# Two more stores whose last two heads go to the first four DMA engines, with the next store held until the other heads have landed

## The chip, the cores and the metric

One core of one Trainium2 chip. The metric is the device time of one execution in microseconds (us). All executions quoted are of the fast state. A ratio is the mean time of one kernel's fast runs over the mean of the other's fast runs of the same rounds on the same chip, so it is not quite the ratio of the medians quoted beside it; intervals are 95%.

## The reference, cut to what matters

```python
# q, k: (16, 512, 16, 64) float32 = batch, sequence, heads, dim; cos, sin: (512, 32)
q_rot = concat([q1*cos - q2*sin, q1*sin + q2*cos])      # the same for k
scores = np.einsum('bshd,bthd->bsht', q_rot, k_rot)     # (16, 512, 16, 512) float32
```

The output is 268 MB and the inputs are 67 MB. The kernel is a long stream of stores with some loads between them.

## The kernel before

The work is cut into 64 steps, four per batch. A step rotates queries and keys (VectorE), transposes them and forms the scores of 128 sequence rows for 16 heads (TensorE), copies them from PSUM into one of three staging buffers of 4 MB (ScalarE), and stores that buffer. SyncE issues all of these transfers. The third and the fourth step of each batch are followed by a load of 2 MB of queries and of keys.

```python
stage_pool = ctx.enter_context(tc.tile_pool(name="stage", bufs=3))
...
    def store(i, st):
        o = o_v[i // C, i % C]
        if i not in (NST - 8, NST - 1):          # NST = 64: steps 56 and 63
            nc.sync.dma_start(o, st)
            return

        h = H - 2
        nc.sync.dma_start(o[:, :h], st[:, :h])
        nc.sync.dma_start(o[:116, h:], st[:116, h:])
        nc.sync.dma_start(o[116:, h:], st[116:, h:])
...
        for i in range(C, NST):
            ...
            st = stage_pool.tile([P, H, S], fp32, tag="stage", name="st")
            for p in range(HP):
                scores(i, p, st)                  # the last of them calls store(i, st)
                ...
            run(dve)
            if i % C == C - 2:
                load("q", i // C + 2)
            elif i % C == C - 1:
                load("k", i // C + 3)
```

A whole store gives each of the 16 DMA engines eight row packets of 32 KB. An **uneven** store gives each engine eight packets of 28 KB (14 heads), then 29 packets of 4 KB to each of the first four engines (116 rows of two heads), then one 4 KB packet to each of the first twelve. I call the 29 packets the four engines' **rest**. It is meant to take load off the slower engines among the other twelve.

Of the kernel before, what the change touches and what calls it, by code (L numbers as in the profile page):

```python
# [10 lines left out]
def kernel(  # L11
# [8 lines left out]
    nc = tc.nc  # L20
# [4 lines left out]
    B, S, H, D = q.shape  # L25
    HD = D // 2
    P = 128
    C = S // P
    HP = H // 2
    NST = B * C  # L30
    G = H // C

    const_pool = ctx.enter_context(tc.tile_pool(name="const", bufs=1))
# [13 lines left out]
    o_v = out.rearrange("b (p c) h t -> b c p h t", c=C)  # L47
# [14 lines left out]
    def load_units(which, head, heads):  # L62
        n = C * heads * D
        t = early[:, used[0] : used[0] + n].rearrange("p (c e) -> p c e", c=C)
        used[0] += n
        src = dram[which][0, :, :, head : head + heads, :]
        nc.sync.dma_start(t.rearrange("p c (h d) -> p c h d", d=D), src)
        for h in range(0, heads, G):
            units[which, (head + h) // G] = t[:, :, D * h : D * (h + G)]

    batches = {}

    def load(which, b):

        if b >= B:
            return
        t = in_pool.tile([P, C, H * D], fp32, tag=which + "_in", name=which + "_sb")
        batches[which, b] = t
        nc.sync.dma_start(t.rearrange("p c (h d) -> p c h d", h=H), dram[which][b])

    def rope(which, n):


        part = part_pool.tile([P, H * D], fp32, tag="part", name="part")
        if n < C:
            x = units[which, n]
            sv, k1, k2 = "p c (g j) -> p c g j", {"j": HD}, {"j": D}
            cs = cos_t.unsqueeze(2).to_broadcast((P, C, 2 * G, HD))
            ss = ss_v.unsqueeze(2).to_broadcast((P, C, G, D))
            pv = part.rearrange("p (c g j) -> p c g j", c=C, j=D)  # L90
            x5 = x.rearrange("p c (h x j) -> p c h x j", x=2, j=HD)
            p5 = part.rearrange("p (c h x j) -> p c h x j", c=C, x=2, j=HD)
            adds = [(x5[:, :, :, y], p5[:, :, :, 1 - y]) for y in range(2)]
        else:
            x = batches[which, n // C][:, n % C]
            sv, k1, k2 = "p (g j) -> p g j", {"j": HD}, {"j": D}
            cs = cos_t[:, n % C].unsqueeze(1).to_broadcast((P, 2 * H, HD))
            ss = ss_v[:, n % C].unsqueeze(1).to_broadcast((P, H, D))
            pv = part.rearrange(sv, **k2)
            x4 = x.rearrange("p (h x j) -> p h x j", x=2, j=HD)  # L100
            swapped = bass.AP(part.tensor, part.offset + HD, [part.ap[0], (D, H), (-HD, 2), (1, HD)])
            adds = [(x4, swapped)]
        xs, xc = x.rearrange(sv, **k2), x.rearrange(sv, **k1)

        def products():
            nc.vector.tensor_tensor(pv, xs, ss, op=mult)  # L106
            nc.vector.tensor_tensor(xc, xc, cs, op=mult)  # L107

        def sums():
            for y, z in adds:  # L110
                nc.vector.tensor_tensor(y, y, z, op=add)  # L111

        return [products, sums]
# [4 lines left out]
    def transposed(which, n, g, copy):  # L118
# [22 lines left out]
                dst = kT[b][:, 4 * g : 4 * g + 4, P * (n % C) : P * (n % C + 1)]  # L141
        copy(out=dst, in_=src)  # L142

    def store(i, st):
        o = o_v[i // C, i % C]
        if i not in (NST - 8, NST - 1):
            nc.sync.dma_start(o, st)
            return

        h = H - 2  # L150
        nc.sync.dma_start(o[:, :h], st[:, :h])
        nc.sync.dma_start(o[:116, h:], st[:116, h:])
        nc.sync.dma_start(o[116:, h:], st[116:, h:])

    def scores(i, p, st):

        ps = ps_s_pool.tile([P, 2, S], fp32, tag="ps_s", name="ps")
        b = i // C
        if b == 0:
            c, hp = divmod(p, 2)  # L160
            lhs, rhs = qT[i][:, C * hp + c], kT[0][:, 2 * i + hp]
        else:
            lhs, rhs = qT[i][:, p], kT[b][:, p]
        for r in range(2):
            po, rh = ps[:, r, :], rhs[64 * r : 64 * r + 64, :]
            nc.tensor.matmul(  # L166
                out=po, lhsT=lhs[64 * r : 64 * r + 64, :], rhs=rh, start=True, stop=True
            )
        so, si = st[:, 2 * p : 2 * p + 2, :], ps
        if b > 0:  # L170
            so = so.rearrange("s r (t c) -> s r t c", c=C)
            si = si.rearrange("s r (c t) -> s r t c", c=C)
        nc.scalar.copy(out=so, in_=si)  # L173
        if b == 0 and p % 2 == 1:
            c = p // 2
            nc.sync.dma_start(o_v[0, c, :, G * i : G * (i + 1)], st[:, G * c : G * (c + 1)])
        elif b > 0 and p == HP - 1:
            store(i, st)

    def tr_act(which, n):  # L180
        for g in range(2):
            transposed(which, n, g, nc.scalar.copy)

    def run(ops):
        for op in ops:
            op()

    with tc.manual_schedule():
        for t, src in ((cos_t, cos), (sin_t, sin)):
            nc.scalar.dma_start(t, src.rearrange("(p c) j -> p c j", c=C))  # L190
        for head, heads in ((0, G), (G, H - G)):
            load_units("k", head, heads)
            load_units("q", head, heads)
        load("k", 1)
        load("q", 1)
        make_identity(nc, ident)
        nc.scalar.copy(out=ss_t[:, :, 0, :], in_=sin_t)
        nc.scalar.mul(ss_t[:, :, 1, :], sin_t, -1.0)
        for which in ("k", "q"):
            run(rope(which, 0))  # L200
            tr_act(which, 0)


        for i in range(C):
            st = st_first[i] if i < 2 else stage_pool.tile([P, H, S], fp32, tag="stage", name="st")
            if i < C - 1:
                dve = rope("k", i + 1) + rope("q", i + 1) + rope("k", C + i)
                nxt = [("k", i + 1), ("q", i + 1)]
            else:
                dve = rope("q", C) + rope("k", C + i) + rope("q", C + 1) + rope("k", 2 * C)  # L210
                nxt = [("q", C), ("k", C + i)]
            for p in range(HP):
                scores(i, p, st)
                if p in (0, 1) and i > 0:
                    run(dve[:1])
                    dve = dve[1:]
                    transposed("k", C + i - 1, p, nc.vector.tensor_copy)
                if p == 3 and i < 2:
                    load("kq"[i], 2)
                if p in (2, 6):  # L220
                    m = len(dve) - (4 if p == 2 else 2) - (2 if i == C - 1 else 0)
                    run(dve[:m])
                    dve = dve[m:]
                    tr_act(*nxt.pop(0))
            run(dve)
        load("k", 3)


        for i in range(C, NST):
            tr = {}  # L230
            if i + 1 < NST:
                tr[1], tr[3] = ("q", i + 1, 0), ("q", i + 1, 1)
            if i + C < NST:
                tr[5], tr[6] = ("k", i + C, 0), ("k", i + C, 1)
            dve = []
            if i + 2 < NST:
                dve += rope("q", i + 2)
            if i + 1 + C < NST:
                dve += rope("k", i + 1 + C)
            st = stage_pool.tile([P, H, S], fp32, tag="stage", name="st")  # L240
            for p in range(HP):
                scores(i, p, st)
                if p not in tr:
                    continue
                if tr[p][0] == "q":
                    run(dve[:1])
                    dve = dve[1:]
                    transposed(*tr[p], nc.vector.tensor_copy)
                else:
                    transposed(*tr[p], nc.scalar.copy)  # L250
            run(dve)
            if i % C == C - 2:
                load("q", i // C + 2)
            elif i % C == C - 1:
                load("k", i // C + 3)


# [28 lines left out]
```

## Time and profile before

| | before |
|---|---|
| time, median of 5 runs beside the changed kernel | 799.13 us (798.6 to 799.73) |
| span of the profiled execution | 799.5 us |
| last landing of step 63's 14 heads, one engine alone | 798.27 us |
| last landing of step 63's rest, four engines | 796.32 us |

The lines of the profile on which the argument rests are shown in the prediction. The last two rows come from the trace's completion records: each engine's share of a transfer has a time of its own, so one can see which share landed first and which last. The profiled execution of the kernel before took 801.33 us in all, 2.2 us above its median. I call the engine that lands last the laggard, and the bunch that lands first the quick engines.

### The profile page before, as it was taken

The page shows a single profiled execution, that of the slowest core. Times are in us where ns is not written, and L with a number is a line of the kernel's source. Part 1 is how long each engine was busy: PE and PEld are TensorE (multiplying, and loading weights), DVE is VectorE, ACT ScalarE, POOL GpSimd, SP SyncE. Part 2 cuts the span into 40 slices and gives each one's busy share as a digit, 9 for nine tenths or more (in the row PEclk, how much of TensorE's full clock was granted, in tenths as well). Part 3 has the DMA queues.
Part 4 walks back from the last instruction along what each step waited for, and adds up shares of the span by engine and source line. Part 5 has one row for each costly group of instructions (what it writes and reads, how often), then busy time and mean ns, then how long its engine had stood idle before and what let it go on. Part 6 is the DMA issues. An engine that isn't in the chain of part 4 may idle for free.

```text
span 799.5 us, 7719 instructions
## 1 busy us (share of the span) xinstructions
PE 688.9 (86%) x3072; PEld 299.3 (37%) x3072; DVE 544.5 (68%) x516; ACT 561.4 (70%) x647; POOL 0.7 (0%) x6
## 2 busy tenths in 40 slices
PE   4989998988979889698897989979979799798970
PEld 2444443433424334243343433424434244343420
DVE  6999987667857667576685766857758577586300
ACT  3888886867848668586685867857757577577870
POOL 0000000000000000000000000000000000000000
PEclk9999999999989989999898989988989889899995
DMA  9999999999999999999999999999999999999996
GB/s 350 423 425 423 434 425 433 424 434 433 420 441 421 439 425 427 436 427 432 428 429 430 434 420 430 425 434 428 403 430 434 436 410 416 430 425 381 422 439 261
DMA packets 17988, 336.17 MB, mean 420 GB/s; under 512 B 1824, under 2 KB 3104, under 8 KB 4384
## 3 DMA queue, kind: packets, MB, share of 16 engines
q1 hardware_dynamic: 17664, 335.55, 98.7%
q8 instruction: 24, 0.39, 0.2%
q10 hardware_dynamic: 288, 0.13, 0.1%
q14 instruction: 12, 0.10, 0.0%
HBM read 67.24 MB, written 268.44 MB: 420 GB/s over the span
## 4 chain that ended last, share of the span: by engine, by line
DMA 48%; PE 38%; DVE 5%; ACT 5%; issue 1%; ACTq 0%; DVEq 0%
DMA out_dram<-st 48%; PE ps L166 28%; PE bank L127 9%; ACT st L173 5%; DVE part L106 2%; DVE early L111 1%; DVE k_sb L111 1%; DVE k_sb L107 1%; DVE early L107 1%; DMA early<-in_k_dram 1%; DVE kT_t L142 0%; DVE q_sb L107 0%; DVE q_sb L111 0%; ACTq L281 0%; DVE qT_t L142 0%
## 5 line engine op out<-in xcount | busy, mean ns | idle before, releaser
L173 ACT COPY st<-ps 128x1024 f32<-128x1024 f32 x512 | 494.8, 1019 | 203.2 <-DMA out_dram<-st 108.6
L166 PE MATMUL ps<-kT_t,qT_t 64*128 64x512 f32 x2048 | 545.8, 650 | 72.5 <-ACT st L173 72.5
L166 PEld LDWEIGHTS ps<-kT_t,qT_t 64*128 64x128 f32 x2048 | 184.5, 197 | 261.3 <-issue 140.3
L142 DVE COPY qT_t<-bank 128x512 f32<-128x512 f32 x118 | 81.5, 691 | 203.9 <-PE bank L127 203.9
L127 PEld LDWEIGHTS bank<-ident,q_sb 128*128 128x128 f32 x480 | 56.0, 153 | 103.1 <-issue 100.5
L127 PE MATMUL bank<-ident,q_sb 128*128 128x128 f32 x480 | 87.6, 310 | 0.9 <-PE ps L166 0.9
L127 PEld LDWEIGHTS bank<-ident,k_sb 128*128 128x128 f32 x480 | 50.5, 141 | 94.3 <-DVE k_sb L107 35.4
L127 PE MATMUL bank<-ident,k_sb 128*128 128x128 f32 x480 | 78.7, 287 | 1.6 <-DVE qT_t L142 1.2
L142 ACT COPY kT_t<-bank 128x512 f32<-128x512 f32 x122 | 72.5, 598 | 6.4 <-PE bank L127 6.4
L107 DVE TENSOR_TENSOR q_sb<-q_sb,cos_t 128x1024 f32<-128x1024 f32 x60 | 73.5, 1225 | 2.1
L107 DVE TENSOR_TENSOR k_sb<-k_sb,cos_t 128x1024 f32<-128x1024 f32 x60 | 73.5, 1225 | 2.0
L111 DVE TENSOR_TENSOR k_sb<-k_sb,part 128x1024 f32<-128x1024 f32 x60 | 73.5, 1225 | 2.1
L106 DVE TENSOR_TENSOR part<-q_sb,ss_t 128x1024 f32<-128x1024 f32 x60 | 73.5, 1225 | 2.0
L106 DVE TENSOR_TENSOR part<-k_sb,ss_t 128x1024 f32<-128x1024 f32 x60 | 72.9, 1215 | 0.1
L111 DVE TENSOR_TENSOR q_sb<-q_sb,part 128x1024 f32<-128x1024 f32 x60 | 72.9, 1215 | 0.0
L127 PE MATMUL bank<-ident,early 128*128 128x128 f32 x64 | 10.5, 316 | 12.3 <-DVE early L111 10.4
L127 PEld LDWEIGHTS bank<-ident,early 128*128 128x128 f32 x64 | 8.3, 161 | 17.4 <-issue 14.8
L106 DVE TENSOR_TENSOR part<-early,ss_t 128x1024 f32<-128x1024 f32 x8 | 9.8, 1222 | 5.8 <-DMA early<-in_k_dram 5.6
L111 DVE TENSOR_TENSOR early<-early,part 128x512 f32<-128x512 f32 x16 | 10.3, 687 | 0.2
L107 DVE TENSOR_TENSOR early<-early,cos_t 128x1024 f32<-128x1024 f32 x8 | 9.8, 1226 | 0.3
L142 ACT COPY qT_t<-bank 128x512 f32<-128x512 f32 x10 | 5.7, 617 | 3.2 <-PE bank L127 3.2
L142 DVE COPY kT_t<-bank 128x512 f32<-128x512 f32 x6 | 4.1, 684 | 0.9 <-PE bank L127 0.9
(9 smaller groups left out, 2.8 us busy)
## 6 DMA issues: line engine op xcount, KB each, us to landing
out_dram<-st SPq DMA_DIRECT2D x58, 4096.0 KB, 24.0
k_sb<-in_k_dram SPq DMA_DIRECT2D x15, 2048.0 KB, 27.9
q_sb<-in_q_dram SPq DMA_DIRECT2D x15, 2048.0 KB, 28.3
out_dram<-st SPq DMA_DIRECT2D x16, 1024.0 KB, 13.5
out_dram<-st SPq DMA_DIRECT2D x2, 3584.0 KB, 23.9
early<-in_k_dram SPq DMA_DIRECT2D x1, 1536.0 KB, 8.7
early<-in_q_dram SPq DMA_DIRECT2D x1, 1536.0 KB, 12.0
out_dram<-st SPq DMA_DIRECT2D x2, 464.0 KB
```

The lines of the kernel that those rows point to most:

```text
L106: nc.vector.tensor_tensor(pv, xs, ss, op=mult)
L107: nc.vector.tensor_tensor(xc, xc, cs, op=mult)
L111: nc.vector.tensor_tensor(y, y, z, op=add)
L127: nc.tensor.transpose(bank[:, x, :], src, ident)
L142: copy(out=dst, in_=src)
L166: nc.tensor.matmul(out=po, lhsT=lhs[64 * r : 64 * r + 64, :], rhs=rh, start=True, stop=True)
L173: nc.scalar.copy(out=so, in_=si)
```

## The change

The intent: relieve the laggard at two more steps, and let the four engines do their rest while the others would wait. Steps 31 and 43 become uneven as well. Their rest is now issued after the load of that step, and the next store (32, 44) is held on SyncE until all shares of the 14-head store have landed. Only SyncE's order of instructions differs.

```diff
+    UNEVEN = (31, 43, 56, NST - 1)
...
+    stores = {}
+    held = mybir.DependencyInfo(mybir.DependencyClass.Sync, mybir.DependencyReason.ANTI)
     def store(i, st):
         o = o_v[i // C, i % C]
-        if i not in (NST - 8, NST - 1):
-            nc.sync.dma_start(o, st)
-            return
-        h = H - 2
-        nc.sync.dma_start(o[:, :h], st[:, :h])
-        nc.sync.dma_start(o[:116, h:], st[:116, h:])
-        nc.sync.dma_start(o[116:, h:], st[116:, h:])
+        h = H - 2 if i in UNEVEN else H
+        stores[i] = nc.sync.dma_start(o[:, :h], st[:, :h])
+        if i - 1 in UNEVEN and i % C == 0 and i < NST - C:
+            tc.add_manual_dep(stores[i].ins, stores[i - 1].ins.name, held, reason="lead")
+    def rest_of_store(i, st):
+        if i in UNEVEN:
+            for rows in (slice(0, 116), slice(116, P)):
+                nc.sync.dma_start(o_v[i // C, i % C, rows, H - 2 :], st[rows, H - 2 :])
...
             elif i % C == C - 1:
                 load("k", i // C + 3)
+            rest_of_store(i, st)
```

## The prediction

> **What bounds the kernel now.** I read the page first (busy shares, slices, DMA queues), then the chain of waits, then windows, then the trace's completion records. The page:
>
> ```profile
> PE 688.9 (86%) x3072; PEld 299.3 (37%) x3072; DVE 544.5 (68%) x516; ACT 561.4 (70%) x647; POOL 0.7 (0%) x6
> DMA  9999999999999999999999999999999999999996
> q1 hardware_dynamic: 17664, 335.55, 98.7%
> q8 instruction: 24, 0.39, 0.2%
> out_dram<-st SPq DMA_DIRECT2D x58, 4096.0 KB, 24.0
> ```
>
> See here: the transfers of queue q1 take 98.7% of the span on the mean of 16 engines, so no compute engine is the bound; only the last slice falls, to six tenths. A mean cannot say which of the 16 ends last. The windows say a little about that (columns: window, length, busy time of PE, PEld, DVE, ACT and POOL, granted clock, DMA share, GB/s):
>
> ```profile
> 500.00:600.00 100.00, 88.42 (x388) 37.78 (x386) 68.78 (x66) 70.14 (x81) 0.00 (x0) 0.91 1.00 424
> 728.00:730.00 2.00, 2.00 (x11) 0.96 (x12) 1.93 (x3) 1.91 (x3) 0.00 (x0) 1.00 0.69 295
> 730.00:732.00 2.00, 2.00 (x12) 0.78 (x8) 1.97 (x2) 1.85 (x4) 0.00 (x0) 1.00 0.42 180
> 732.00:734.00 2.00, 2.00 (x14) 1.00 (x12) 1.17 (x3) 1.61 (x2) 0.00 (x0) 1.00 1.12 475
> ...
> 792.00:794.00 2.00, 0.00 (x0) 0.00 (x0) 0.00 (x0) 0.00 (x0) 0.00 (x0) 0.50 0.40 150
> 794.00:796.00 2.00, 0.00 (x0) 0.00 (x0) 0.00 (x0) 0.00 (x0) 0.00 (x0) 0.50 0.33 119
> 796.00:798.00 2.00, 0.00 (x0) 0.00 (x0) 0.00 (x0) 0.00 (x0) 0.00 (x0) 0.50 0.04 18
> ```
>
> See the one large hole, at 728 to 732 us, and the tail: at 792 to 794 us 0.40 of 16, some six engines, still move data; at 796 to 798 us 0.04, one engine. So the time is set by the **slowest single engine**, not by the mean. The chain of waits shows how the program follows it:
>
> ```profile
> 399.67 0.33 SPq L147 DMA_DIRECT2D out_dram<-st  x1
> 400.11 0.98 SPq L79 DMA_DIRECT2D k_sb<-in_k_dram  x1
> 409.69 24.49 SPq L147 DMA_DIRECT2D out_dram<-st  x3
> ...
> 409.69 28.29 DMA out_dram<-st
> 437.98 0.02 issue
> 438.00 0.04 ACTq L173
> ```
>
> The first three lines are SyncE's timeline (store of step 31, load of keys, store of step 32 and two more), the rest the chain: a store is issued at 409.69, its last share lands at 437.98, and only then does ScalarE get that staging buffer back.
>
> The completion records hold a time for each engine's share of a transfer. For the store of step 31: first share at 413.86 us, last at 423.05; in order, 0.0 0.0 0.0 0.0 0.1 0.5 0.6 0.7 0.9 1.2 2.2 4.4 5.3 5.7 7.8 9.2 us after the first. Eleven engines run nearly together and five lag, the last by 9.2 us. This spread was 0.7 us at the early loads, 4.4 at step 4, 11.5 at step 42, and 11.8 at step 56. The laggard is never without work; the eleven begin to be: their landings against an unbroken sum of packets slip by 0.4 us near 516, 1.7 near 561, 2.1 near 660, and over 4 us at the hole of 728 to 732, where they wait for the store of step 58.
>
> **What the Trainium skill says.** "DMA: Bandwidth & Descriptors", section "Why a DMA increments its semaphore by 16 and not by 1": a transfer is spread over the largest k up to 16 that divides its slowest dimension, and from SyncE these are the lowest-numbered k. 116 rows give k = 4 (29 rows each), 12 rows give k = 12. The trace agrees: 4 and 12 completions. Same page, "Anatomy of one DMA": waits are made by the issuing sequencer, the engines just consume their queues; so the new hold blocks SyncE only, and queued transfers go on. The trace agrees: after a dry spell, the store issued at 731.80 lands first at 742.75, which is eight packets of 1.21 us and 1.25 us to start and report. "Runtime: NRT & Kernel Launch", "Instruction fetch mechanics": instructions come in 16 KiB blocks over a DMA queue of their own. The trace agrees: q8 moves 24 such blocks, some 0.94 us each, on whichever engines; part of why engines are unequal.
>
> **The change, part by part.** Nothing moves on PE, VectorE or ScalarE; the order of instructions differs on SyncE alone, by four more issues (116 and 12 rows, twice, behind the load of that step) and a wait before the stores of steps 32 and 44. Steps 56 and 63 were uneven already.
>
> *For the twelve others, the laggard among them.* A row packet of 32 KB takes 1.213 us, one of 28 KB 1.062, one of 4 KB 0.159. One uneven store: 8 x 0.151 = 1.21 us less, for the laggard one 4 KB packet more, so -1.04. (Of the twelve completions for 12 rows at step 56, the last came at 729.9, behind its other shares, so the laggard is among engines 4 to 11.) Twice: **-2.1 us on the laggard**, whose last landing moves from 798.46 to 796.4.
>
> *For the first four.* 29 x 0.159 = 4.61, plus 0.17 for the twelfth rows and semaphores, less 1.21: +3.6 us, twice **+7.2 us**. At step 56 their four landings came 4.66, 4.8, 5.2 and 6.0 us after the first main landing: they are among the quick eleven, but one is 1.3 us behind. Now they finish at 796.65. Their slack is what they idle: 0.4 + 1.7 + 2.1 = 4.2 us, and at most 0.6 us at 728 to 732 (there they still had step 56's rest to do, ending store 57 at 732.4 to 733.8 against data at 733.05). 796.65 + 7.2 - 4.2 = **799.6 us**, 1.2 us after the present end of 798.46.
>
> *The hold.* The slow share of store 31 now lands at 423.05 - 1.2 = 421.9; store 32 is then issued and its data flows at about 423.1. The laggard still has 4.85 us of keys until 426.9: no hole for it, with 3.8 us to spare. The quick ones without rest are done at 418.7 - 1.2 = 417.5 and idle 5.6 us, which costs nothing as they are ahead by more. The four run their rest from 417.5 to 422.4 (the hindmost to 423.6) and idle 0.7 us at most. At step 43 the lead is smaller, the four run past the release and idle nothing. The 12-row packet behind the keys gives buffer 31 back at 427.0 instead of 423.05, so step 34's store goes from 433.9 to about 437.9; two stores, some 19 us, are queued then, so this is hidden.
>
> Sum: the end is the later of laggard (796.4) and the four (799.6), against 798.46: +1.2 us, and 799.13 + 1.2 = 800.3 us.
>
> **Rivals.** (1) *The laggard stays the bound*: the four keep up because they idle more before than I count. Then the whole -2.1 us comes through: 797.0 us. For it: the end of the run before is a lone engine from 796.7 on, and the change is visibly meant for this. Against: the four need 7.2 us and I find under 5. (2) *The four become the bound*, my sum: 800.3, up to 802 if the hindmost of them, which idled less, decides, or if the laggard is less slow in unprofiled executions (the profiled one took 801.33 us against 799.13), so that there is less to win. (3) *The hold opens a hole on all 16*: for it, the late buffer 31 and a store issued 12 us later; against, the 3.8 us to spare and 19 us in queue. If a hole opens it is some 2 to 4 us each time: 803 to 807. (4) All cancels, since the two ends differ by a few us and laggards wander: 799.
>
> **Range and chances.** I give (1) 0.35, (2) 0.4, (4) 0.2, (3) 0.05. 0.35 x 797.0 + 0.4 x 800.6 + 0.2 x 799.1 + 0.05 x 805 = 799.2; I take 799.4. Eight in ten: 796.9 to 801.6. Two per cent are 16 us; every term here is under 8 us, so faster 0.005, same 0.985, slower 0.01.
>
> **What would show each step.** Completions: two more sets of four some 4.7 us after the quick landings of that step, near 422 and 573 us. The spread of landings should fall from about 9.5 to some 4 after step 32, from 10 to 4 after step 44. A hole in the DMA share just before 423 and near 570 us, of about 7 engines. The hole at 728 to 732 should shrink, and the small ones near 561 and 660 vanish. The chain should still run over store landings, and SyncE should wait some 13 us more at the store of step 32. In the tail, look at who ends last: if four engines carry the last microseconds, (2) is right; if one alone does, at about 796, (1). I would be wrong if the four are not among the quick engines on that chip, if the laggard runs dry after the hold, or if the laggard is another one in each run.

## The result, and the profile after

The changed kernel takes **806.75 us** (806.08 to 808.49, 5 runs) against 799.13: ratio 1.010, interval 1.0085 to 1.0115. That is within 2%, but 7 us above the predicted time and 5 us above the range.

The page of the changed kernel, the lines that answer to those of before:

```profile
PE 685.9 (85%) x3072; PEld 297.3 (37%) x3072; DVE 544.5 (68%) x516; ACT 561.2 (70%) x647; POOL 0.7 (0%) x6
DMA  9999999999999999999999999999999999999995
q1 hardware_dynamic: 17952, 335.55, 98.1%
```

The compute engines do what they did, and the DMA engines are busy almost all the time on the mean. The page cannot tell where 7 us went. SyncE's timeline (start, length, instruction), its waits, and the chain of waits around the first hold:

```profile
397.51 0.33 SPq L151 DMA_DIRECT2D out_dram<-st  x1
397.95 0.76 SPq L80 DMA_DIRECT2D k_sb<-in_k_dram  x1
399.16 0.71 SPq L160 DMA_DIRECT2D out_dram<-st  x2
423.12 16.73 SPq L151 DMA_DIRECT2D out_dram<-st  x3
```
```profile
SPq L151 <- DMA out_dram<-st: 44.5, 2, 23.2
```
```profile
399.55 28.73 DMA out_dram<-st
428.28 0.02 issue
428.31 0.04 ACTq L180
```

Store 31 and its rest (two issues at 399.16) are out, and SyncE then stands still until 423.12. The two holds together are 44.5 us of waiting, the longest 23.2. The chain now runs over the 12-row packet behind the keys: the staging buffer comes back at 428.28 instead of 423.05.

The windows around the hold and around the old hole (window, length, busy time of PE, PEld, DVE, ACT, POOL, clock, DMA share, GB/s), first the changed kernel, then the kernel before where the prediction does not show it:

```profile
419.00:421.00 2.00, 2.00 (x12) 0.72 (x8) 1.34 (x2) 0.17 (x1) 0.00 (x0) 1.00 0.59 231
421.00:423.00 2.00, 0.47 (x4) 0.00 (x0) 1.28 (x2) 0.00 (x0) 0.00 (x0) 1.00 0.18 74
423.00:425.00 2.00, 0.00 (x0) 0.00 (x0) 0.00 (x0) 0.00 (x0) 0.00 (x0) 0.65 0.64 270
...
728.00:730.00 2.00, 2.00 (x13) 0.91 (x13) 1.93 (x3) 1.86 (x3) 0.00 (x0) 1.00 1.02 420
730.00:732.00 2.00, 2.00 (x10) 0.91 (x12) 1.00 (x1) 1.86 (x3) 0.00 (x0) 1.00 1.02 420
```
```profile
419.00:421.00 2.00, 2.00 (x14) 0.84 (x12) 1.31 (x3) 0.69 (x1) 0.00 (x0) 1.00 1.07 459
421.00:423.00 2.00, 0.99 (x4) 0.16 (x4) 1.79 (x2) 0.00 (x0) 0.00 (x0) 1.00 0.93 401
```

The hold makes a hole at 419 to 425 us (share down to 0.18, against 0.93 before). The hole at 728 to 732 us, 0.69 and 0.42 before, is not smaller but **gone**: 1.02.

The tail of the changed kernel:

```profile
796.00:798.00 2.00, 0.00 (x0) 0.00 (x0) 0.00 (x0) 0.00 (x0) 0.00 (x0) 0.50 0.27 104
798.00:800.00 2.00, 0.00 (x0) 0.00 (x0) 0.00 (x0) 0.00 (x0) 0.00 (x0) 0.50 0.22 63
800.00:802.00 2.00, 0.00 (x0) 0.00 (x0) 0.00 (x0) 0.00 (x0) 0.00 (x0) 0.50 0.24 96
802.00:804.00 2.00, 0.00 (x0) 0.00 (x0) 0.00 (x0) 0.00 (x0) 0.00 (x0) 0.50 0.14 55
```

A share of 0.24 of 16 is four engines. The kernel before ended with one engine (0.04). The transfers of the last stretch, 799.6 to 804 us:

```profile
DMA packets 88, 0.33 MB, mean 74 GB/s; under 512 B 8, under 2 KB 8, under 8 KB 88
```

All 88 packets are under 8 KB: nothing is left but the last rest. In the completion records, the 14 heads of step 63 land at 791.51 to 799.43 (790.51 to 798.27 before), and the rest lands at **802.70 to 803.97** (795.74 to 796.32 before). The four engines set the end, 7 us later than they did.

**Where the quick engines idle.** I compared the first share of each store with an unbroken sum of the packet times up to it (32 KB 1.213 us, 28 KB 1.062, a 16 KB load packet 0.611). Where the difference grows, the quickest engines were idle or slow. Growth in us, by stretch of steps:

| profiled execution | 31 to 33 (first hold) | 33 to 35 | 42 to 45 (second hold) | 45 to 47 | 47 to 56 | 56 to 59 |
|---|---|---|---|---|---|---|
| before | -0.1 | -0.1 | 1.6 | -0.1 | 1.9 | **5.7** |
| changed | **7.6** | 1.8 | 2.6 | 2.0 | -0.2 | **0.3** |

The hold did not only add idle time; it took it away from steps 56 to 59. There, in the kernel before, the four engines ran the rest of step 56 (4.8 us: 29 packets of 0.159 and 0.17 for the rest's end) while the quick engines had nothing to do. Theory P (for place) says: *a rest is free only as far as the quick engines idle at that very place; the hold moves the idle time, so it uncovers the rest of step 56.*

### The profile page after: what moved, and what is told of

Its sections match the earlier page's. It is cut to its first block, busy times and chain, and to the rows that moved or that the text cites. A ratio compares the mean times of both kernels' runs of the same rounds, so it can differ in the third digit from the quotient of the medians.

```text
span 805.0 us, 7725 instructions
## 1 busy us (share of the span) xinstructions
PE 685.9 (85%) x3072; PEld 297.3 (37%) x3072; DVE 544.5 (68%) x516; ACT 561.2 (70%) x647; POOL 0.7 (0%) x6
## 3 DMA queue, kind: packets, MB, share of 16 engines
q1 hardware_dynamic: 17952, 335.55, 98.1%
## 4 chain that ended last, share of the span: by engine, by line
DMA 49%; PE 37%; DVE 5%; ACT 5%; issue 1%; ACTq 0%; SPq 0%
DMA out_dram<-st 48%; PE ps L173 28%; PE bank L128 9%; ACT st L180 5%; DVE part L107 2%; DVE early L112 1%; DVE k_sb L108 1%; DVE k_sb L112 1%; DVE early L108 1%; DMA sin_t<-in_sin_dram 0%; DVE kT_t L143 0%; DVE q_sb L108 0%; DVE q_sb L112 0%; ACTq L289 0%; SPq L160 0%
## 5 line engine op out<-in xcount | busy, mean ns | idle before, releaser
L128 PE MATMUL bank<-ident,q_sb 128*128 128x128 f32 x480 | 85.9, 306 | 0.9 <-PE ps L173 0.9
L128 PE MATMUL bank<-ident,early 128*128 128x128 f32 x64 | 10.5, 316 | 12.3 <-DVE early L112 10.4
```

Of the source, the lines that this page charges most:

```text
L128: nc.tensor.transpose(bank[:, x, :], src, ident)
```

## The experiments

All results are correct. Diffs are against the changed kernel. "Before" beside the runs: 799.69 us (e1 to e4), 799.75 (e5 to e8), 800.46 (e9 to e12), 799.47 (e13 to e15). The texts of expectation use these names: F and F2, the four engines' load decides the end; H, the hold decides it. The others are rivals that the texts describe.

| run | uneven steps | held | median us | ratio (95%) |
|---|---|---|---|---|
| changed | 31, 43, 56, 63 | 32, 44 | 806.75 | 1.010 (1.0085 to 1.0115) |
| e1 | 31, 43, 56, 63 | none | 810.86 | 1.0135 (1.0116 to 1.0154) |
| e2 | 56, 63 | 32, 44 | 807.01 | 1.0089 (1.0069 to 1.0108) |
| e3 | 31, 43, 63 | 32, 44 | 802.49 | 1.003 (1.0011 to 1.0048) |
| e4 | 31, 43, 63 | none | 806.07 | 1.0073 (1.0058 to 1.0089) |
| e5 | as changed, rest ahead of load | 32, 44 | 809.78 | 1.0125 (1.0098 to 1.0151) |
| e6 | as changed, rest ahead of load | none | 805.17 | 1.0077 (1.0046 to 1.0108) |
| e7 | none | 32, 44 | 803.51 | 1.0045 (1.003 to 1.006) |
| e8 | 63 | none | 800.99 | 1.0012 (0.9997 to 1.0027) |
| e9 | as changed, 31 and 43 split over all 16 | 32, 44 | 807.49 | 1.0094 (1.0075 to 1.0113) |
| e10 | as changed, 31 and 43 split over all 16 | none | 803.41 | 1.0048 (1.0028 to 1.0069) |
| e11 | 31, 56, 63, rest ahead of load | none | 803.4 | 1.0038 (1.0018 to 1.0058) |
| e12 | 43, 56, 63, rest ahead of load | none | 803.52 | 1.0037 (1.0014 to 1.0059) |
| e13 | 31, 63 | 32, 44 | 801.04 | 1.0021 (1.0006 to 1.0036) |
| e14 | 31, 56, 63 | 32, 44 | 806.0 | 1.0079 (1.0064 to 1.0094) |
| e15 | 31, 63 | 32 | 800.86 | 1.0021 (1.0004 to 1.0038) |

### e1: the uneven stores without the hold

```diff
-        if i - 1 in UNEVEN and i % C == 0 and i < NST - C:
-            tc.add_manual_dep(stores[i].ins, stores[i - 1].ins.name, held, reason="lead")
```

> The changed kernel without the two holds: all four uneven stores stay. Theory F (the four engines that carry the 116 rows end last; the holds make them idle 1.4 to 3 us and line all engines up, which makes the next turn from stores to loads slow, 3.8 us in two places): most of that comes back, about 800 to 802 us, the four engines still last. Theory H (the holds alone are the cost, the moved rows a gain of 2.1 us on the laggard): about 797 us. If the moved rows alone are the cost: still 806 us.

Measured: 810.86 us, worse than with the hold, which no theory had. Chain and windows of this run (columns as above):

```profile
545.54 30.38 DMA out_dram<-st
575.92 0.02 issue
```
```profile
584.00:586.00 2.00, 2.00 (x14) 0.91 (x12) 1.93 (x3) 1.86 (x3) 0.00 (x0) 1.00 0.72 311
586.00:588.00 2.00, 2.00 (x11) 1.02 (x12) 1.18 (x1) 1.85 (x3) 0.00 (x0) 1.00 0.50 213
588.00:590.00 2.00, 2.00 (x12) 0.88 (x10) 0.58 (x1) 1.97 (x3) 0.00 (x0) 1.00 0.65 279
```

Buffer 43 comes back with the last piece of its rest at 575.92, while its 14 heads had landed at 567.98. The rest queues behind 2 MB of keys, so the step that needs this buffer is late, its store (46) goes out at 588.16 (581.04 before), and the engines run dry: share 0.50. What follows: issuing the rest behind the load makes the buffer late, and this is not hidden.

### e2: the hold alone

```diff
-    UNEVEN = (31, 43, 56, NST - 1)
+    UNEVEN = (56, NST - 1)
-        if i - 1 in UNEVEN and i % C == 0 and i < NST - C:
+        if i - 1 in (31, 43):
```

> The kernel before with the stores of steps 32 and 44 held until those of 31 and 43 have landed, all of these stores whole. Theory F: the four engines have 7.2 us less to do than in the changed kernel, so they are not the bound; the laggard has work queued through the hold, so about 799 to 801 us. Theory H: the holds cost what they cost there, about 806 us.

Measured: 807.01 us, near H's 806 and as slow as the changed kernel, though the four engines carry no more than before. Its old hole and its tail:

```profile
728.00:730.00 2.00, 2.00 (x14) 0.95 (x12) 1.93 (x3) 1.91 (x3) 0.00 (x0) 1.00 0.91 373
...
798.00:800.00 2.00, 0.00 (x0) 0.00 (x0) 0.00 (x0) 0.00 (x0) 0.00 (x0) 0.50 0.25 78
800.00:802.00 2.00, 0.00 (x0) 0.00 (x0) 0.00 (x0) 0.00 (x0) 0.00 (x0) 0.50 0.24 96
```

The hole is nearly gone and four engines end last, at 801.99 to 803.44. So the hold makes the loss even without more load on the four, and F in its plain form falls. How the hold does it, this run alone does not say.

### e3 and e4: without the rest of step 56

```diff
-    UNEVEN = (31, 43, 56, NST - 1)
+    UNEVEN = (31, 43, NST - 1)
```
(e4: also without the hold, as in e1.)

> The changed kernel with its holds, but the store of step 56 whole: the four engines carry 3.6 us less. Theory F: they end 3.6 us earlier, about 803 us. Theory H: step 56 has no hold, so nothing comes back: 806.7 us or, with the laggard 1 us longer, 807.7 us.

> Uneven at 31, 43 and 63, no hold: one more uneven store than before, none held. Theory F: the four engines carry 3.6 us more than before and idle that much less, the laggard 1.04 us less: 797.5 to 799 us. Theory H (each uneven store without a hold gains 1.04 us): 798.1 us. Faster than e1 under F, slower than e1 by 1 us under H.

Measured: 802.49 with the hold, 4.3 us less than the changed kernel; 806.07 without it, 4.8 less than e1 and above every expectation. In both pairs, the rest of step 56 costs most of its 4.8 us or all of it. In the kernel before it does not (e8). The six runs of e3 fall into two groups, 800.7 to 801.1 and 803.9 to 804.7 us; the profiled one is of the slower group.

### e5 and e6: the rest ahead of the load

```diff
             run(dve)
+            rest_of_store(i, st)
             if i % C == C - 2:
...
-            rest_of_store(i, st)
```
(e6: also without the hold.)

> The changed kernel, holds kept, with the 116 and 12 rows issued ahead of that step's load of keys, so that the staging buffer comes back some 5 us earlier. Theory F2 (the four engines end last; they carry 7.2 us more than before and idle about as much as before, by the holds and by slow turns from stores to loads after engines have been lined up): the buffer was not what they waited for when held, so 805 to 808 us, as the changed kernel. Rival B (the late buffer is the cost): about 800 us.

> The same order, without the holds. e1 (no hold, rest behind the load) took 810.9 us: there the buffers of steps 31 and 43 came back at 425.7 and 575.9 us, up to 8 us after the last share of the main store, and the engines ran dry by 3.3 and 5.2 us before the stores of steps 34 and 46. Theory F2: with the rest first the buffers come back about 5 us earlier and half or more of that dry time goes: 803 to 806 us. If the late buffer is not the cause in e1: 810 us again.

Measured: 809.78 held, above the ranges of both theories; 805.17 not held, within F2's. Without the hold, moving the rest ahead of the load takes 5.7 us off e1 (4.6 by the ratios, as the two ran on different chips): about the price of the late buffers that e10 gives below. With the hold it is no help.

### e7 and e8: the hold with all stores even; the uneven store of step 63 alone

```diff
-    UNEVEN = (31, 43, 56, NST - 1)
+    UNEVEN = ()                       # e7, and the hold's condition as in e2
+    UNEVEN = (NST - 1,)               # e8, and no hold
```

> Both holds, and no uneven store at all. Theory F2: the four engines carry 7.2 us less than in e2 (807.0 us), so they no longer end last; the laggard does, with 2.1 us more than in e2, where its last main share landed at 799.3 us: last landing about 801.5 us, some 803 to 804 us in all, faster than e2. Theory H (a hold stops all engines, the laggard too): 2 us slower than e2, 809 us.

> The kernel before with only its last store uneven, no hold. If the laggard sets the end of the kernel before, as its trace shows, it has 1.04 us more to do: about 800.5 us against 799.5, and the four engines end some 3 us before it. If the four set it already: faster than before by up to 3 us.

Measured: e7 803.51, in F2's range and not in H's; e8 800.99, near what was expected. The tail of e7:

```profile
796.00:798.00 2.00, 0.00 (x0) 0.00 (x0) 0.00 (x0) 0.00 (x0) 0.00 (x0) 0.50 0.08 33
798.00:800.00 2.00, 0.00 (x0) 0.00 (x0) 0.00 (x0) 0.00 (x0) 0.00 (x0) 0.50 0.08 33
800.00:802.00 2.00, 0.00 (x0) 0.00 (x0) 0.00 (x0) 0.00 (x0) 0.00 (x0) 0.50 0.00 0
```

One engine, the laggard, carries the end (0.08 of 16). It ends at 801.10, about where it should without the relief of two uneven stores: 798.27 and twice 1.04 is 800.35. So in this trace the hold hardly delays the laggard. By the medians e7 is 3.8 us above the kernel before, of which the missing relief explains 2.1; up to 1.7 us may be the hold's. Making steps 56 and 63 uneven under the hold (e7 to e2) makes the kernel *slower* by 3.5 us, though it relieves the laggard. And e8 against the kernel before is the uneven store of step 56 without a hold: leaving it out changes the time by 0.12%, which is not clear of noise (the interval reaches below 1), and the four's last landing only from 796.32 to 795.68. So there the rest costs next to nothing.

### e9 and e10: at steps 31 and 43 the two heads split over all 16 engines

```diff
-            for rows in (slice(0, 116), slice(116, P)):
+            cut = 112 if i < NST - 8 else 116
+            for rows in (slice(0, cut), slice(cut, P)):
```
(112 rows are seven to each engine, 16 rows one to each. e10: also without the hold.)

> The changed kernel with its holds, but at steps 31 and 43 the two heads are left to 112 and 16 rows, which spread over all 16 engines (7 rows and 1 row each): the same number of transfers, no imbalance. Theory F2 (the hold's idle time and the four engines' rows share the same gap): the four have 7.2 us less to do but idle through the hold, as in e2 (807.0 us): 805 to 808 us. Rival I (the imbalance is the cost, held or not): 800 us.

> The same even split without the holds, to be set against e1 (116 and 12 rows, no hold: 810.9 us). Theory F2: without imbalance and without hold only the later return of two buffers remains (some 5 us, by the load of keys ahead of the rest), which makes the quick engines run dry for some 3 us: 800 to 802.5 us. Rival T (the extra transfers themselves, or the late buffers alone, are the cost in e1): 806 to 811 us.

Measured: 807.49 held, in F2's range and as slow as the changed kernel, so taking the load of steps 31 and 43 off the four gains nothing under the hold. Not held: 803.41, between the ranges of F2 and T. There the four carry nothing new, so 0.48%, some 4 us, is the late buffers (store 34 at 439.02, store 46 at 586.99), with the two extra transfers per step, which no run takes apart from them.

### e11 and e12: one more uneven store, rest ahead of the load, no hold

```diff
-    UNEVEN = (31, 43, 56, NST - 1)
+    UNEVEN = (31, 56, NST - 1)        # e11
+    UNEVEN = (43, 56, NST - 1)        # e12
```

> An attempt at a faster kernel: uneven at 31, 56 and 63, rest ahead of the load, no hold. The four engines carry 3.6 us more than in the kernel before, the laggard 1.04 us less. Theory F2: if the four make up for it out of their idle time, the laggard's gain shows: 798.7 us at best; if they do not, they end up to 3.6 us later than 796.65 plus their own luck: up to 802 us. I expect 800.5 us.

> As e11 with step 43 in place of 31. The four engines have had some idle time by then in the kernel before, so less is left to absorb the rows: the same or slower than e11, 799 to 802.5 us. A kernel faster than before by 1 us would speak for the laggard as the bound even with three uneven stores.

Measured: 803.4 (800.15 to 805.55) and 803.52 (800.22 to 806.33), above the ranges given and with a wide spread from run to run; the kernel before spread too in these rounds (798.82 to 802.45). Neither beats the kernel before. In the profiled execution of e11 the quick engines idle by under 0.2 us between steps 31 and 35 and the four end at 796.20 to 801.06.

### e13, e14 and e15: tests of theory P

By now F2 had missed e5, e10, e11 and e12, and had met e9 only with e2's time put into it; "the hold costs 7 us" did not fit e7. Theory P was formed on those runs, so it needed runs of its own.

```diff
-    UNEVEN = (31, 43, 56, NST - 1)
+    UNEVEN = (31, NST - 1)            # e13 and e15
+    UNEVEN = (31, 56, NST - 1)        # e14
-        if i - 1 in UNEVEN and i % C == 0 and i < NST - C:
+        if i - 1 in (31, 43):         # e13 and e14
+        if i - 1 == 31:               # e15
```

> Both holds kept, rests at 31 and 63 only (43 and 56 even). Theory P, place: a rest is free only as far as the quick engines idle just there; total idle is set by the pace, the hold only moves it (quick engines idle 7.6 us at store 32, 2.6 at store 44 and 0.3 at 56 to 58 in the changed kernel; nothing, 1.6 and 5.7 before). Rest 31 lies in the 5 to 7 us of the first hold, so nothing of it shows: the four end at the first main landing of step 63 (about 790.5 to 792) plus 4.8, behind by up to 2, 795.5 to 798.5; a lone laggard ends, at 799.3 as with the hold alone and two rests: 801 to 803 us. Rival S, the hold itself costs 7 us on the four wherever rests lie (as the hold alone seemed to say): 805.5 to 808, four engines last. Rival F2, the four's load alone: 797 for the four, 800 to 802.

> As the last, and the rest of step 56 too. Theory P: quick engines idle under 0.5 us at 56 to 58, so 4.5 of its 4.8 us show: the four end 4 to 5 us later than in the last, 800.5 to 803, and are the end; 803.5 to 806 us, at least 2 us above the last. Rival S: 805.5 to 808, no difference between the two. Rival F2: the four 3.6 later than in the last, 800.5, time 801.5 to 803.

> As e13 with the first hold alone. Theory P: less idle is taken early, so part of the hole at 56 to 58 comes back (2 to 4 us), where nothing uses it; a lone laggard ends: 800 to 802.5 us. Rival S: half the hold, 802.5 to 805. It is also the version that I would hope to match the kernel before.

Measured: 801.04, 806.0 and 800.86, each in the range that P gave (e14 at its upper end). S is outside for e13 and e15; e14 lies in its range too, but S had no difference between e13 and e14. F2 holds e13 (800 to 802) and misses e14 (801.5 to 803). The windows of e13, then of e14:

```profile
796.00:798.00 2.00, 0.00 (x0) 0.00 (x0) 0.00 (x0) 0.00 (x0) 0.00 (x0) 0.50 0.04 16
798.00:800.00 2.00, 0.00 (x0) 0.00 (x0) 0.00 (x0) 0.00 (x0) 0.00 (x0) 0.50 0.00 0
```
```profile
796.00:798.00 2.00, 0.00 (x0) 0.00 (x0) 0.00 (x0) 0.00 (x0) 0.00 (x0) 0.50 0.20 59
798.00:800.00 2.00, 0.00 (x0) 0.00 (x0) 0.00 (x0) 0.00 (x0) 0.00 (x0) 0.50 0.23 88
800.00:802.00 2.00, 0.00 (x0) 0.00 (x0) 0.00 (x0) 0.00 (x0) 0.00 (x0) 0.50 0.12 39
```

In e13 one engine is left at the end, in e14 up to four. The only edit between them is the uneven store of step 56, and it costs 5.0 us by the medians. In the profiled executions the four's last landing moves by 6.7 us, 796.07 to 802.81; the first 2.0 of them lie before the laggard's end in e13 (798.06) and do not show. Without a hold, the same edit (e8 to the kernel before) moved the four by 0.6 us. The idle table again, with sums from step 31 to 63:

| profiled execution | 31 to 33 | 42 to 45 | 56 to 59 | sum | four end | worked out |
|---|---|---|---|---|---|---|
| before | -0.1 | 1.6 | 5.7 | 9.5 | 795.7 to 796.3 | 795.3 |
| changed | 7.6 | 2.6 | 0.3 | 13.7 | 802.7 to 804.0 | 803.0 |
| e2 | 5.3 | 2.3 | 0.2 | 10.5 | 802.0 to 803.4 | 800.5 |
| e3 | 4.9 | 2.7 | -0.1 | 10.4 | 796.2 to 801.1 | 797.1 |
| e7 | 5.4 | 1.9 | -0.1 | 10.0 | no rest | |
| e8 | -0.1 | 0.3 | 5.9 | 8.2 | 794.9 to 795.7 | 794.4 |
| e13 | 4.8 | 2.4 | -0.1 | 9.8 | 795.1 to 796.1 | 795.3 |
| e14 | 4.4 | 2.2 | 0.4 | 9.6 | 800.3 to 802.8 | 799.1 |
| e15 | 4.5 | -0.2 | 3.0 | 8.6 | 794.6 to 795.5 | 794.5 |

The last column is theory P's sum: the first landing of step 63's 14 heads, 4.8 us for its own rest, and of each earlier rest what the idle time at its place leaves uncovered. For the changed kernel: 791.5 + 4.8 + 0 (step 31: 4.8 under 7.6) + 2.2 (step 43: 4.8 less 2.6) + 4.5 (step 56: 4.8 less 0.3) = 803.0. It fits within 1.3 us in the kernel before, the changed kernel, e8, e13 and e15. In e2, e3 and e14 the hindmost of the four is up to 4 us later than that; some of them trail the quickest by a few us already. With the hold the sum of idle time in this table is much as before (9.6 to 10.5 where no more than one rest is added, 8.2 to 9.5 unheld): the **place** changes. With half the hold (e15), 3.0 us of the old hole come back.

The runs that the table leaves out fit less well. In e5 and e9 the hindmost of the four lands 6.4 and 6.3 us after the sum. In e1, e4, e6, e10, e11 and e12 it is within 3 us of it, but the first of the four can be 6 us before it. And e1 with e4 shows a limit of P: the quick engines of e1 idle 5.5 us at steps 56 to 59, yet the rest of step 56 costs 4.8 us there. In e1 the four come to step 56 already late: the rest of that step lands at 728.67 to 735.04 (722.57 to 723.88 in the kernel before), buffer 56 comes back at 735.23, and store 59 goes out at 744.41 (738.32 in e4), so that part of this idle time comes from the rest itself. It seems that idle time of the quick engines is room for a rest only while the four keep up with them; no run isolates this. P tells at which place a rest shows; its sum is rough.

## Why the prediction was wrong, by its own steps

- **The step that failed: the four's slack, -4.2 us.** The prediction took what the four idled in the kernel before as given, counted the rest of step 56 as already hidden in the hole at 728 to 732 us, and let two more rests eat the idle time elsewhere: +7.2 - 4.2. But the hold moves that hole to 419 to 425 us. The rest of step 31 is hidden there in full, that of step 43 lacks 2.2 us, and that of step 56, hidden before, now shows with 4.5. The four's end moved by 803.97 - 796.32 = 7.65 us (7.0 for the first of them), where the prediction had 3.0. That e13 and e14 differ by 5.0 us, and e8 and the kernel before by no more than noise, shows that the place decides.
- **"[The hold] costs nothing as they are ahead by more": wrong for the whole.** The hold alone gives 807.01 us (e2). It was right for the laggard, whose queue did not run dry. Yet being ahead was what had opened the hole that hid step 56's rest.
- **The size of the hold.** The quick engines idle 7.6 us there (5.6 predicted), and at 421 to 423 us a share of 0.18 leaves some 13 of the 16 without work (7 predicted). The four idle too, some 1.2 to 2.7 us and not "0.7 us at most": their last 4 KB packets end at 421.2 to 422.8 us, the data of store 32 starts at 424.0.
- **The late buffer, "hidden" by 19 us of queued stores: wrong for the kernel without the hold**, where it costs some 4 us (e10). Under the hold I have no run that isolates it.
- **The laggard, -2.1 us: not seen.** Its last share of step 63 lands at 799.43, 1.16 us later than before. In the profiled execution the laggard was already 11.2 us behind at step 31 (9.2 before), so its lag differs between executions by as much as the term.
- **Rivals.** Rival 2 (the four become the bound) named the right engines, but too small a size. Rival 3 had a size that fits, 803 to 807, for another reason: the hole is not one on all 16 engines at the hold. It had 0.05. Rivals 1 and 4 fell.
- **What was right:** the hold blocks SyncE alone (the laggard's load of keys runs on and lands at 428.08, 5.0 us after its share of store 31); two more sets of four completions; the spread of landings down to 4.06 us after store 32 and 3.76 after store 44; the tail of four engines as the mark of rival 2. "The hole at 728 to 732 should shrink" was right as well, and there the prediction had the key in hand: it did not ask who lived in that hole.

What stays open: why the laggard's lag and the four's order differ between executions; how the loss of e5 over the changed kernel (3 us) arises; why the four end so late in e9; and the slow load after each hold, below. None of the fifteen versions beat the kernel before; e8, e13 and e15 come within about 0.2% of it.

## What to carry to other kernels

Idle time of an engine that is ahead may be the room in which other work is hidden. Before a wait is moved, list what runs in the holes that it will close, and count that work as uncovered. And where 16 engines drift apart, follow the engine that ends last by its own completions: the mean busy share (98.7% and 98.1% here, some 789 us of each span) says that no work was added, and not who ends last.

## What the Trainium skill lacked or had wrong

- "DMA: Bandwidth & Descriptors", section "Why a DMA increments its semaphore by 16 and not by 1", says that the engines of a transfer finish independently. It does not say how far they drift when stores are queued without a wait: here from 0.7 us at the early loads to 11.8 us at step 56, and that a wait for all shares brings this down to 4 us.
- The same page, section "Where 436 GB/s comes from", gives 358 GB/s as what binds between HBM and SBUF. Here one core moves 424 GB/s over 100 us (the prediction's window 500 to 600), so for a core alone that sentence is wrong, and the page's 435 is the nearer limit. The same passage does note a measurement of 425.
- No page tells of a load that is slow after the engines were lined up. In the same stretch at the first turn from stores to a load, before and then changed:

```profile
452.00:459.00 7.00, 7.00 (x36) 3.01 (x33) 6.48 (x6) 6.19 (x8) 0.00 (x0) 1.00 1.01 433
```
```profile
452.00:459.00 7.00, 7.00 (x36) 3.13 (x34) 6.18 (x7) 6.19 (x8) 0.00 (x0) 1.00 1.00 328
```

  The DMA engines are as busy, but move 328 GB/s in place of 433: 7 x (433 - 328) / 433 = 1.7 us. The same 1.6 to 2.0 us appear after each hold in e2, e3, e7, e9, e13 and e14, and neither in the kernel before and e8 (-0.1 to 0.0) nor where e15 has no hold (-0.1). No run isolates the cause.
- "Runtime: NRT & Kernel Launch", section "Instruction fetch mechanics", calls the cost of crossing a block "mostly hidden". It does not say that the fetches (24 of 16 KB here, some 0.94 us each) take time from the engines that carry the data. The trace does not name their engine, but after most of them one share falls back: in the kernel before from 4.2 to 5.6 us behind the first at step 47 (fetch at 606.80) and from 3.7 to 5.1 at step 50 (fetch at 641.48). The laggard is another matter: it loses 0.2 to 0.3 us at most stores, fetch or not. What the fetches cost the whole kernel no run shows.
